# Modulation sums over 128 columns, and a new order of the first steps, in a decoder trunk

## Chip, cores and metric

One core of one Trainium2 chip. The metric is the device time of one execution in microseconds (us), as the median over runs.

## What is computed

One layer of a decoder trunk over 512 positions of 1024 channels: a modulated RMS norm, one input projection that feeds two attention branches, a gated merge, then a second modulated norm and a gated MLP. The change touches only the beginning, the modulated norm and the first 768 columns of the projection:

```python
cs = jax.nn.silu(c)
mod = cs @ w_ada[l] + b_ada[l]
shift1, scale1, gate1, shift2, scale2, gate2 = [m[:, None, :] for m in jnp.split(mod, 6, axis=-1)]
h = _rmsnorm(x, norm1_g[l]) * (1.0 + scale1) + shift1
proj = h @ w_in[l]
```

Here `x` is 512 x 1024, `c` is 1 x 1024, `w_ada` is 1024 x 6144 and `w_in` is 1024 x 4352, all float32. So each of the 1024 channels needs one scale and one shift before it can go into the projection, and each of these is a sum over 1024 products of `cs` with a column of `w_ada`.

## The kernel before

The 1024 channels are cut into eight blocks of 128, k = 0 to 7, and each block is one step. For a step the kernel needs `mod` (a scale and a shift for each of the 128 channels), the modulated tile `h` (128 channels x 512 positions), and the block's 128 x 768 weights. To keep float32 accuracy in a fast format, both operands are split into a high and a low part. `hTh` and `hTl` are the parts of `h`; `w0h` and `w0l` are those of the weights. A step multiplies high by high, low weight by high, and high by low `h`, for each of six output blocks (the six PSUM accumulators `acc6`).

*TensorE's order.* The instructions of TensorE, VectorE and ScalarE in this stage run in the order in which the program writes them (a manual schedule, L243). `mm_k(k, 0)` (L385) does the twelve products that need `hTh`; `mm_k(k, 2)` does the six that need `hTl`. Between them stands the work for the next step: reducing the modulation sums (`reduce_mod`, L314), transposing the next block of `x` (`h_turn`, L367), finishing `mod` (`finish_mod`, L325) and making the next `hTh` and its float32 copy `hf` (`h_tile`, L372). In step 1 the six products of `mm_k(1, 2)` are split in two halves of three, with the next step's work in between (L478).

*How a modulation sum is made.* `adaw[k]` holds the block of `w_ada` of step k: index j = 0 for the scale and j = 1 for the shift, and eight column blocks kk of 128 inputs. There are two ways. `direct` (L295) multiplies on TensorE: the 128 x 128 block of `adaw` is the weight, one column of `cs` is the moving operand, and the result is one column of PSUM. The other way runs on VectorE: `ac_first` (L272) and `ac_ops` (L281) multiply the blocks by their `cs` value and add them up, elementwise over 128 x 256, into two accumulators `ac` (even and odd kk), which are added at last. `reduce_mod` then sums `ac` over the partitions with a product by a column of ones.

Step 0 uses `direct` for all of the scale and for half of the shift; the other half of the shift, `a0`, is summed on VectorE (L434 to L438). Step 1 does kk = 6 and 7 directly (`early_mod`, L305) into columns 2 and 3 of a PSUM tile, VectorE adds these to the biases (`part`, L311), and the rest comes by `ac`. Steps 2 to 7 go all by `ac`. The `ac` of step k+1 is made while step k's products run.

*VectorE's list within a step* is: `ac_ops` for the next step with `h_low` (L382, which makes `hTl`) at some place in it, then `finish_mod`, then the two instructions of `split_lo` (L357, which make `w0l` of the next step). `ac_first` runs on ScalarE, apart from the odd one of step 2.

*Warmers.* `keep_warm(n)` (L254) multiplies the identity by ones into an accumulator that is overwritten later. It takes n x 128 columns, up to 512 in one product. Its only purpose is to keep TensorE busy.

*Loads.* SP's queue holds all loads of this stage in program order (L225): four tiles of `x` of 512 KB, then for each step the two 512 KB halves of `adaw` (in four pieces of 256 KB for steps 1 and 2) and 384 KB of `w_in`. Buffers of `adaw` are used again three or two steps later, so the issues of the last steps wait until VectorE has read the old contents. After this stage come further loads for the projections and for the rest of the modulation (`ra`, L834).

Of the kernel before, what the change touches and what calls it, by code (L numbers as in the profile page):

```python
# [39 lines left out]
DIFF_FILL = (3, 2, 4, 2)  # L40
WARM_EARLY = 5
WARM = 10
GROUPS = ((0,), (1,), (2,), (3,), (4,), (5,), (6,), (7,))
MOD_AT = 2

COL_KA = 512
COL_VA = 640
# [8 lines left out]
def kernel(  # L56
# [142 lines left out]
    p1 = ExitStack()  # L199
    pp = pool("p1", stack=p1)  # L200
    xn = pp.tile([P, NT, D], F32, name="xn")
    groups = GROUPS
    adaw, w0 = {}, {}

    def load_ada(g):
        k, m = g[0], len(g)
        if k % 3 == 2:
            aw = big.tile([P, 2, KT, m * P], F32, tag="out" + "hl"[k // 3], name=f"adaw{k}")
        else:
            aw = pp.tile([P, 2, KT, m * P], F32, tag="adaw", bufs=2, name=f"adaw{k}")  # L210
        cut = 4 if k in (1, 2) else KT
        for a in range(0, KT, cut):
            for j, base in ((0, D), (1, 0)):
                nc.sync.dma_start(
                    aw[:, j, a : a + cut],
                    wada[a * P : (a + cut) * P, base + k * P : base + (k + m) * P].rearrange("(a p) n -> p a n", p=P),
                )
        adaw[k] = aw

# [5 lines left out]
    with tc.manual_schedule(engines={nc.sync.engine}):  # L225
        for t in range(NT):
            nc.sync.dma_start(xn[:, t], xd[t * P : (t + 1) * P, :])
        load_ada(groups[0])
        load_w0(0)
        for k in range(1, KT):  # L230
            load_ada(groups[k])
# [38 lines left out]


    def ac_first(gi, b):  # L272
        a = pp.tile([P, 2, len(groups[gi]) * P], F32, tag=f"ac{b}", bufs=2, name=f"ac{gi}_{b}")
        aw = adaw[groups[gi][0]]
        if gi == 2 and b:
            nc.vector.tensor_scalar_mul(a, aw[:, :, b], cs[:, b : b + 1])
        else:
            nc.scalar.activation(a, aw[:, :, b], AF.Copy, scale=cs[:, b : b + 1])
        ac.setdefault(gi, {})[b] = a

    def ac_ops(gi, low):  # L281
        aw = adaw[groups[gi][0]]
        order = (3, 2, 5, 4) if gi == 1 else (3, 2, 5, 4, 7, 6)
        if gi == 2:
            ac_first(2, 1)
        for n, kk in enumerate(order):
            if n == (2, 4)[gi > 1] and gi < 3:
                low()
            a = ac[gi][kk % 2]
            nc.vector.scalar_tensor_tensor(a, aw[:, :, kk], cs[:, kk : kk + 1], a, ALU.mult, ALU.add)  # L290
        nc.vector.tensor_add(ac[gi][0], ac[gi][0], ac[gi][1])
        if gi > 2:
            low()

    def direct(pa, j, c, k, kks, stop=True):  # L295
        for kk in kks:
            nc.tensor.matmul(
                pa[:, c : c + 1],
                adaw[k][:, j, kk],
                cs[:, kk : kk + 1],  # L300
                start=kk == kks[0],
                stop=stop and kk == kks[-1],
            )

    def early_mod(gi):  # L305
        pa = tbank(f"pa{gi}", (P, 4))
        for c, j in ((2, 1), (3, 0)):
            direct(pa, j, c, gi, (6, 7))
        part = pp.tile([P, 2], F32, name="part")
        both = cols[:, 0:16].rearrange("p (a b) -> p b a", a=2)  # L310
        nc.vector.tensor_add(part, pa[:, 2:4], both[:, gi])  # L311
        return pa, part

    def reduce_mod(gi, early=None):  # L314
        pas = []
        for i, k in enumerate(groups[gi]):
            pa = early[0] if early else tbank(f"pa{k}", (P, 2))
            for j in range(2):
                nc.tensor.matmul(
                    pa[:, j : j + 1], ac[gi][0][:, j, i * P : (i + 1) * P], ones[:, 0:1], start=True, stop=True  # L320
                )
            pas.append(pa)
        return pas

    def finish_mod(gi, pas, early=None):  # L325
        for k, pa in zip(groups[gi], pas):
            m = pp.tile([P, 16], F32, tag="mod", bufs=3, name=f"mod{k}")
            sh, sc = (early[1][:, 0:1], early[1][:, 1:2]) if early else (bsh[:, k : k + 1], bsc1[:, k : k + 1])
            last = nc.vector.scalar_tensor_tensor(m[:, 0:1], pa[:, 0:1], sc, n1g[:, k : k + 1], ALU.add, ALU.mult)
            if gi:  # L330
                nc.scalar.activation(m[:, 1:2], pa[:, 1:2], AF.Identity, bias=sh)
            else:
                nc.vector.tensor_add(m[:, 1:2], pa[:, 1:2], sh)
            mods[k] = m
        return last

    def w0_views(k):
# [34 lines left out]
    def h_tile(k):  # L372
        hf = pp.tile([P, S], F32, tag="hf", bufs=2, name=f"hf{k}")
        for dst in (hTh[k], hf):
            nc.scalar.activation(dst, pts[k], AF.Identity, bias=mods[k][:, 1:2], scale=mods[k][:, 0:1])
            if dst is not hf and k < 2:
                if k == 0:
                    ac_first(1, 1)
                ac_first(k + 1, 0)
        hfs[k] = hf  # L380

    def h_low(k):  # L382
        nc.vector.tensor_sub(hTl[k], hfs[k], hTh[k].bitcast(F32))

    def mm_k(k, part, some=DONE):  # L385
        wh, wl = wts[k]
        last = k == KT - 1
        if part == (2 if last else 1):
            return
        for i in some:  # L390
            for p in (1, 2) if last and part else (0, 1) if part == 0 and not last else (part,):
                lhs, rhs = ((wh, hTh), (wl, hTh), (wh, hTl))[p]
                nc.tensor.matmul(  # L393
                    acc6[i], lhs[:, i * P : (i + 1) * P], rhs[k], start=k == 0 and p == 0, stop=last and p == 2
                )
# [25 lines left out]
    pa0 = tbank("pa0", (P, 2))  # L421
# [16 lines left out]
    nc.tensor.matmul(pa0[:, 1:2], a0, ones[:, 0:1], start=False, stop=True)  # L438
# [10 lines left out]
    for gi, g in enumerate(groups):  # L449
        nxt = groups[gi + 1] if gi + 1 < len(groups) else ()  # L450

        for k in nxt:
            split_hi(k)

        if nxt:
            ac_ops(gi + 1, lambda: h_low(g[0]))
        else:
            h_low(g[0])
        if not nxt:
# [12 lines left out]
        for k in g:  # L472
            if k == 0:
                h_turn(1)
            for part in range(3):
                part_2 = DONE
                if part == MOD_AT and k == g[-1] and nxt:
                    if gi == 1:  # L478
                        mm_k(k, part, DONE[:3])
                        part_2 = DONE[3:]  # L480
                    early = early_mod(1) if gi == 0 else None
                    pas = reduce_mod(gi + 1, early)
                    if gi and gi + 2 < len(groups):
                        ac_first(gi + 2, 1)
                        ac_first(gi + 2, 0)
                    if len(nxt) == 1 and gi:
                        h_turn(nxt[0])
                    last_mod = finish_mod(gi + 1, pas, early)
                    for n in nxt:
                        split_lo(n, 0)  # L490
                        split_lo(n, 1)
                    for n in nxt:
                        if len(nxt) > 1:
                            h_turn(n)
                        h_tile(n)
                mm_k(k, part, part_2)
            if k == g[0]:
                for n in g[1:]:
                    h_low(n)
    man.close()  # L500
    p1.close()

# [1410 lines left out]
```

## Time and profile before

| | us |
|---|---|
| runs shown | 696.82, 699.29, 698.24 |
| median of them | 698.24 |
| the profiled execution, whole | 697.19 |
| its span on the core | 695.1 |

The page of the profile gives a busy time for each engine (PE is TensorE, PEld its weight loads, DVE VectorE, ACT ScalarE, POOL GpSimd, SP the queue that issues loads). A row of a timeline begins with the start and the length in us, then comes the engine, the line of the kernel, the operation, the tile written and the tiles read, the shape, and the number of instructions merged into the row. In brackets stands how long the engine was idle before, and what ended that. A float32 product appears as two records, one of a float32r operand as one. The granted clock is the share of full speed that the chip gave TensorE.

### The profile page before, as it was taken

The page shows a single profiled execution, that of the slowest core. Times are in us where ns is not written, and L with a number is a line of the kernel's source. Part 1 is how long each engine was busy: PE and PEld are TensorE (multiplying, and loading weights), DVE is VectorE, ACT ScalarE, POOL GpSimd, SP SyncE. Part 2 cuts the span into 40 slices and gives each one's busy share as a digit, 9 for nine tenths or more (in the row PEclk, how much of TensorE's full clock was granted, in tenths as well). Part 3 has the DMA queues.
Part 4 walks back from the last instruction along what each step waited for, and adds up shares of the span by engine and source line. Part 5 has one row for each costly group of instructions (what it writes and reads, how often), then busy time and mean ns, then how long its engine had stood idle before and what let it go on. Part 6 is the DMA issues. An engine that isn't in the chain of part 4 may idle for free.

```text
span 695.1 us, 11259 instructions
## 1 busy us (share of the span) xinstructions
PE 683.7 (98%) x4203; PEld 593.3 (85%) x4203; DVE 567.6 (82%) x1073; ACT 382.7 (55%) x687; POOL 82.9 (12%) x100
## 2 busy tenths in 40 slices
PE   8999999999999999999999999999999999999995
PEld 4787877777788888888889999999999999888885
DVE  4799987887885557663789998888888999979997
ACT  6666675544552333332468756655555666655665
POOL 3000000000101000000030111111111102540300
PEclk9999999999999999999999999999999999999998
DMA  9984454454435676339817788787889648997903
GB/s 308 344 237 155 150 158 146 127 165 116 140 92 171 194 218 203 98 99 284 279 37 147 152 202 196 165 197 200 196 220 227 159 132 216 191 202 199 167 1 121
DMA packets 115926, 121.81 MB, mean 175 GB/s; under 512 B 4447, under 2 KB 93344, under 8 KB 115872
## 3 DMA queue, kind: packets, MB, share of 16 engines
q1 hardware_dynamic: 96958, 95.09, 43.6%
q0 software_dynamic: 18720, 25.73, 22.0%
q8 instruction: 33, 0.54, 0.3%
q10 hardware_dynamic: 194, 0.28, 0.1%
q14 instruction: 21, 0.17, 0.1%
HBM read 118.97 MB, written 2.11 MB: 174 GB/s over the span
## 4 chain that ended last, share of the span: by engine, by line
PE 91%; DVE 3%; DMA 3%; ACT 1%; issue 1%; SPq 0%; POOLq 0%; ACTq 0%; DVEq 0%
PE up L1242 32%; PE dc L1857 15%; PE a L393 4%; PE pgd L123 2%; PE oc L1298 2%; PE oc L1302 2%; PE pgd L125 2%; PE pgd L124 2%; PE oc L1299 2%; DMA ra<-in_w_ada_dram 2%; PE pga L123 2%; PE pga L125 2%; PE pga L124 2%; PE pw L123 1%; PE pk L123 1%; PE pk L125 1%
## 5 line engine op out<-in xcount | busy, mean ns | idle before, releaser
L1242 PE MATMUL up<-t,m_whi 128*128 128x256 f32 x512 | 93.1, 283 | 0.0
L1242 PEld LDWEIGHTS up<-t,m_whi 128*128 128x128 f32 x512 | 79.9, 192 | 0.0
L1242 PE MATMUL up<-t,m_wlo 128*128 128x256 f32 x256 | 72.4, 283 | 0.0
L1242 PE MATMUL up<-bh,p_whi 128*128 128x256 f32 x232 | 65.7, 283 | 0.0
L1242 PE MATMUL up<-bl,p_whi 128*128 128x256 f32 x232 | 65.7, 283 | 0.0
L1242 PE MATMUL up<-bh,p_wlo 128*128 128x256 f32 x232 | 65.7, 283 | 0.0
L858 DVE SCALAR_TENSOR_TENSOR arow<-ra,cs,arow 128x512 f32<-128x512 f32 x56 | 41.9, 749 | 21.6 <-DMA ra<-in_w_ada_dram 21.0
L1242 PEld LDWEIGHTS up<-t,m_wlo 128*128 128x128 f32 x256 | 49.2, 192 | 0.0
L1242 PEld LDWEIGHTS up<-bh,p_whi 128*128 128x128 f32 x232 | 44.5, 192 | 0.0
L1242 PEld LDWEIGHTS up<-bl,p_whi 128*128 128x128 f32 x232 | 44.5, 192 | 0.0
L1242 PEld LDWEIGHTS up<-bh,p_wlo 128*128 128x128 f32 x232 | 44.5, 192 | 0.0
L1151 POOL DMA_DIRECT2D s<-in_w_up_dram x21 | 27.0, 1361 | 139.6 <-DMA s<-in_w_up_dram 69.2
L1179 ACT CAST m_whi<-s 128x1024 fp32r<-128x1024 f32 x31 | 32.4, 1047 | 11.1 <-DVE s L1173 7.7
L1183 DVE TENSOR_TENSOR m_wlo<-s,m_whi 128x1024 fp32r<-128x1024 f32 x31 | 37.7, 1217 | 0.0
L1242 PE MATMUL up<-t,p_whi 128*128 128x256 f32 x176 | 32.2, 283 | 0.0
L877 POOL DMA_DIRECT2D mod_rows<-row x8 | 5.1, 643 | 197.0 <-ACT row L876 197.0
L177 POOL TENSOR_TENSOR r<-ms,mhalf 128x1 f32<-128x1 f32 (+1 forms) x16 | 13.1, 822 | 127.6 <-DVE ms L175 72.8
L772 ACT ACTIVATE sd<-sd,dmx 128x128 f32<-128x128 f32 (+3 forms) x32 | 17.7, 557 | 19.0 <-DVE dmx L764 18.9
L1242 PEld LDWEIGHTS up<-t,p_whi 128*128 128x128 f32 x176 | 27.5, 192 | 0.0
L1249 ACT ACTIVATE gT<-a,cv 128x512 f32<-128x512 f32 x22 | 17.7, 813 | 16.9 <-DVE a L1284 15.8
L1179 ACT CAST p_whi<-wa 128x1024 fp32r<-128x1024 f32 x18 | 18.7, 1041 | 12.6 <-PE up L1242 12.6
L1183 DVE TENSOR_TENSOR p_wlo<-wa,p_whi 128x1024 fp32r<-128x1024 f32 x18 | 22.0, 1220 | 3.8 <-ACT p_whi L1179 3.2
(491 smaller groups left out, 2077.9 us busy)
## 6 DMA issues: line engine op xcount, KB each, us to landing
ra<-in_w_ada_dram SPq DMA_DIRECT2D x32, 512.0 KB, 4.1
wa<-in_w_up_dram SPq DMA_DIRECT2D x22, 512.0 KB, 4.1
s<-in_w_up_dram SPq DMA_DIRECT2D x21, 512.0 KB, 4.6
s<-in_w_up_dram POOLq DMA_DIRECT2D x21, 512.0 KB, 6.7
adaw<-in_w_ada_dram SPq DMA_DIRECT2D x12, 512.0 KB, 6.5
w<-in_w_in_dram SPq DMA_DIRECT2D x12, 512.0 KB, 4.6
a<-in_w_up_dram SPq DMA_DIRECT2D x11, 512.0 KB, 4.5
b<-in_w_down_dram SPq DMA_DIRECT2D x10, 512.0 KB, 4.0
```

The lines of the kernel that those rows point to most:

```text
L123: nc.tensor.matmul(o, lh, rh, start=start, stop=False)
L124: nc.tensor.matmul(o, lh, rl, start=False, stop=False)
L125: nc.tensor.matmul(o, ll, rh, start=False, stop=stop)
L393: nc.tensor.matmul(acc6[i], lhs[:, i * P : (i + 1) * P], rhs[k], start=k == 0 and p == 0, stop=last and p == 2)
L772: exp = nc.scalar.activation(pm[m], pm[m], AF.Exp, bias=mx[:, m : m + 1], scale=slope, accum_out=lsum[:, m : m + 1])
L858: nc.vector.scalar_tensor_tensor(ac, r[:, a], cc, ac, ALU.mult, ALU.add)
L1151: nc.gpsimd.dma_start(dst, upblock(*blk), accum_op=ALU.add)
L1179: nc.scalar.copy(W[J, name][0], R[J, SRC[name]])
L1183: nc.vector.tensor_sub(lo, R[J, SRC[name]], hi.bitcast(F32))
L1242: nc.tensor.matmul(o[u], w[:, k, cu], b[:, k], start=name in ("p1", "m5", "p2") and k == 0 and x == 0, stop=k == 3 and x == 2, skip_group_ ...
L1249: nc.scalar.activation(grow(j), av[J][:, u], AF.Identity, bias=cv[:, 66 + j : 67 + j], scale=cv[:, 44 + j : 45 + j])
L1857: nc.tensor.matmul(bank2[u][:, sl], a[:, q, cu], b[:, q, sl], start=first_mm and x == 0, stop=last_mm and x == 2, skip_group_check=name no ...
```

## The change

Four things are done. First, `direct` uses its column of `cs` 128 times over (a broadcast, so the same column is read again), and the result is 128 equal columns of PSUM, of which the first is used; the same holds for `a0` and for step 1's reduction, which now multiply by all 128 columns of `ones`. Second, step 1's direct products and its reduction accumulate in the same PSUM columns, so `part` goes away. Third, step 0's direct products are laid out otherwise on TensorE: three of them ahead of the third transpose, five behind it and ahead of the fourth; and the warmer behind them has 256 columns instead of 512. Fourth, VectorE's list of the first steps: the odd `ac_first` of step 1 moves there from ScalarE; `w0l` of step 1 is made ahead of `finish_mod(1)`; in step 2's sums the order of kk is 3, 5, 2, 7, 4, 6, and `h_low(1)` comes behind them. With that, `mm_k(1, 2)` is no longer split in halves. The general case of steps with more than one block (`GROUPS`), which was not in use, is taken out.

```diff
     def ac_first(gi, b):
...
-        if gi == 2 and b:
+        if gi in (1, 2) and b:
             nc.vector.tensor_scalar_mul(a, aw[:, :, b], cs[:, b : b + 1])
...
     def ac_ops(gi, low):
-        aw = adaw[groups[gi][0]]
-        order = (3, 2, 5, 4) if gi == 1 else (3, 2, 5, 4, 7, 6)
-        if gi == 2:
-            ac_first(2, 1)
+        aw = adaw[gi]
+        if gi < 3:
+            ac_first(gi, 1)
+        order = {1: (3, 2, 5, 4), 2: (3, 5, 2, 7, 4, 6)}.get(gi, (3, 2, 5, 4, 7, 6))
         for n, kk in enumerate(order):
-            if n == (2, 4)[gi > 1] and gi < 3:
+            if gi == 1 and n == 2:
                 low()
...
-        if gi > 2:
+        if gi > 1:
             low()
...
-    def direct(pa, j, c, k, kks, stop=True):
+    def direct(pa, j, k, kks, start=True, stop=False):
         for kk in kks:
             nc.tensor.matmul(
-                pa[:, c : c + 1],
+                pa[:, j],
                 adaw[k][:, j, kk],
-                cs[:, kk : kk + 1],
-                start=kk == kks[0],
+                cs[:, kk : kk + 1].to_broadcast([P, P]),
+                start=start and kk == kks[0],
                 stop=stop and kk == kks[-1],
             )
...
     def early_mod(gi):
-        pa = tbank(f"pa{gi}", (P, 4))
-        for c, j in ((2, 1), (3, 0)):
-            direct(pa, j, c, gi, (6, 7))
-        part = pp.tile([P, 2], F32, name="part")
-        both = cols[:, 0:16].rearrange("p (a b) -> p b a", a=2)
-        nc.vector.tensor_add(part, pa[:, 2:4], both[:, gi])
-        return pa, part
+        pa = tbank(f"pa{gi}", (P, 2, P))
+        direct(pa, 0, gi, (6, 7))
+        return pa
...
     def reduce_mod(gi, early=None):
...
+        pa = early or tbank(f"pa{gi}", (P, 2, P))
+        for j in range(2):
+            if early:
+                if j:
+                    direct(pa, 1, gi, (6, 7))
+                nc.tensor.matmul(pa[:, j], ac[gi][0][:, j], ones, start=False, stop=True)
             else:
...
+                nc.tensor.matmul(pa[:, j, 0:1], ac[gi][0][:, j], ones[:, 0:1], start=True, stop=True)
+        return pa
...
         if t:
             normalise(t - 1)
+            if t == 3:
+                direct(pa0, 0, 0, range(3))
             turn(t - 1)
             if t < 3:
                 keep_warm(4)
     normalise(NT - 1)
-    direct(pa0, 0, 0, 0, range(7), False)
+    direct(pa0, 0, 0, range(3, 8), start=False, stop=True)
     turn(NT - 1)
-    nc.tensor.matmul(pa0[:, 0:1], adaw[0][:, 0, 7], cs[:, 7:8], start=False, stop=True)
...
-    direct(pa0, 1, 1, 0, range(4), False)
-    nc.tensor.matmul(pa0[:, 1:2], a0, ones[:, 0:1], start=False, stop=True)
-    finish_mod(0, [pa0])
+    direct(pa0, 1, 0, range(4))
+    nc.tensor.matmul(pa0[:, 1], a0, ones, start=False, stop=True)
+    finish_mod(0, pa0)
...
-    keep_warm(4)
+    keep_warm(2)
     h_tile(0)
...
         for dst in (hTh[k], hf):
             nc.scalar.activation(dst, pts[k], AF.Identity, bias=mods[k][:, 1:2], scale=mods[k][:, 0:1])
             if dst is not hf and k < 2:
-                if k == 0:
-                    ac_first(1, 1)
                 ac_first(k + 1, 0)
...
+        mm_k(gi, 0)
+        mm_k(gi, 1)
+        if more:
+            if gi == 0:
+                split_lo(1, 0)
+                split_lo(1, 1)
+            pa = reduce_mod(gi + 1, early_mod(1) if gi == 0 else None)
+            if gi and gi + 2 < KT:
+                ac_first(gi + 2, 1)
+                ac_first(gi + 2, 0)
+            if gi:
+                h_turn(gi + 1)
+            last_mod = finish_mod(gi + 1, pa)
+            if gi:
+                split_lo(gi + 1, 0)
+                split_lo(gi + 1, 1)
+            h_tile(gi + 1)
+        mm_k(gi, 2)
```

More of the change, by code (lines that the diff above doesn't have):

```diff
@@ L201, with load_ada @@
     xn = pp.tile([P, NT, D], F32, name="xn")
-    groups = GROUPS
     adaw, w0 = {}, {}
-    def load_ada(g):
-        k, m = g[0], len(g)
+    def load_ada(k):
         if k % 3 == 2:
-            aw = big.tile([P, 2, KT, m * P], F32, tag="out" + "hl"[k // 3], name=f"adaw{k}")
+            aw = big.tile([P, 2, KT, P], F32, tag="out" + "hl"[k // 3], name=f"adaw{k}")
         else:
-            aw = pp.tile([P, 2, KT, m * P], F32, tag="adaw", bufs=2, name=f"adaw{k}")
+            aw = pp.tile([P, 2, KT, P], F32, tag="adaw", bufs=2, name=f"adaw{k}")
         cut = 4 if k in (1, 2) else KT
@@ L215, in load_ada @@
                     aw[:, j, a : a + cut],
-                    wada[a * P : (a + cut) * P, base + k * P : base + (k + m) * P].rearrange("(a p) n -> p a n", p=P),
+                    wada[a * P : (a + cut) * P, base + k * P : base + (k + 1) * P].rearrange("(a p) n -> p a n", p=P),
                 )
@@ L227 @@
             nc.sync.dma_start(xn[:, t], xd[t * P : (t + 1) * P, :])
-        load_ada(groups[0])
+        load_ada(0)
         load_w0(0)
         for k in range(1, KT):
-            load_ada(groups[k])
+            load_ada(k)
             load_w0(k)
@@ L272, in ac_first @@
     def ac_first(gi, b):
-        a = pp.tile([P, 2, len(groups[gi]) * P], F32, tag=f"ac{b}", bufs=2, name=f"ac{gi}_{b}")
-        aw = adaw[groups[gi][0]]
-        if gi == 2 and b:
+        a = pp.tile([P, 2, P], F32, tag=f"ac{b}", bufs=2, name=f"ac{gi}_{b}")
+        aw = adaw[gi]
+        if gi in (1, 2) and b:
             nc.vector.tensor_scalar_mul(a, aw[:, :, b], cs[:, b : b + 1])
@@ L281, in ac_ops @@
     def ac_ops(gi, low):
-        aw = adaw[groups[gi][0]]
-        order = (3, 2, 5, 4) if gi == 1 else (3, 2, 5, 4, 7, 6)
-        if gi == 2:
-            ac_first(2, 1)
+        aw = adaw[gi]
+        if gi < 3:
+            ac_first(gi, 1)
+        order = {1: (3, 2, 5, 4), 2: (3, 5, 2, 7, 4, 6)}.get(gi, (3, 2, 5, 4, 7, 6))
         for n, kk in enumerate(order):
-            if n == (2, 4)[gi > 1] and gi < 3:
+            if gi == 1 and n == 2:
                 low()
@@ L305, in early_mod, with finish_mod @@
     def early_mod(gi):
-        pa = tbank(f"pa{gi}", (P, 4))
-        for c, j in ((2, 1), (3, 0)):
-            direct(pa, j, c, gi, (6, 7))
-        part = pp.tile([P, 2], F32, name="part")
-        both = cols[:, 0:16].rearrange("p (a b) -> p b a", a=2)
-        nc.vector.tensor_add(part, pa[:, 2:4], both[:, gi])
-        return pa, part
-    def reduce_mod(gi, early=None):
[L315 to L331, printed above, removed]
-            else:
-                nc.vector.tensor_add(m[:, 1:2], pa[:, 1:2], sh)
-            mods[k] = m
+        pa = tbank(f"pa{gi}", (P, 2, P))
+        direct(pa, 0, gi, (6, 7))
+        return pa
+    def reduce_mod(gi, early=None):
+        pa = early or tbank(f"pa{gi}", (P, 2, P))
[4 more added lines that the diff above has]
+                nc.tensor.matmul(pa[:, j], ac[gi][0][:, j], ones, start=False, stop=True)
+            else:
+                nc.tensor.matmul(pa[:, j, 0:1], ac[gi][0][:, j], ones[:, 0:1], start=True, stop=True)
+        return pa
+    def finish_mod(k, pa):
+        m = pp.tile([P, 16], F32, tag="mod", bufs=3, name=f"mod{k}")
+        last = nc.vector.scalar_tensor_tensor(
+            m[:, 0:1], pa[:, 0, 0:1], bsc1[:, k : k + 1], n1g[:, k : k + 1], ALU.add, ALU.mult
+        )
+        if k:
+            nc.scalar.activation(m[:, 1:2], pa[:, 1, 0:1], AF.Identity, bias=bsh[:, k : k + 1])
+        else:
+            nc.vector.tensor_add(m[:, 1:2], pa[:, 1, 0:1], bsh[:, k : k + 1])
+        mods[k] = m
         return last
@@ L383, in h_low, with mm_k @@
         nc.vector.tensor_sub(hTl[k], hfs[k], hTh[k].bitcast(F32))
-    def mm_k(k, part, some=DONE):
+    def mm_k(k, part):
         wh, wl = wts[k]
@@ L389, in mm_k @@
             return
-        for i in some:
+        for i in DONE:
             for p in (1, 2) if last and part else (0, 1) if part == 0 and not last else (part,):
@@ L419, in scale_x @@
         nc.scalar.activation(xn[:, t, HEAD:], xn[:, t, HEAD:], AF.Copy, scale=rst[:, t : t + 1])
-    pa0 = tbank("pa0", (P, 2))
+    pa0 = tbank("pa0", (P, 2, P))
     for t in range(NT):
@@ L447 @@
     split_lo(0, 1)
[L449 to L456, printed above, removed]
-        else:
-            h_low(g[0])
-        if not nxt:
+    for gi in range(KT):
+        more = gi + 1 < KT
+        if more:
+            split_hi(gi + 1)
+            ac_ops(gi + 1, lambda: h_low(gi))
+        else:
+            h_low(gi)
             lp = cpool.tile([P, 2, 64], F32, name="lp")
@@ L470 @@
             nc.vector.tensor_scalar_add(nlam, nlam, -LAM_INIT)
[L472 to L499, printed above, removed]
+        if gi == 0:
+            h_turn(1)
+        mm_k(gi, 0)
+        mm_k(gi, 1)
+        if more:
+            if gi == 0:
+                split_lo(1, 0)
[12 more added lines that the diff above has]
+        mm_k(gi, 2)
     man.close()
```

2 lines of the change are left out of this document (removed).

## The prediction

> **What bounds the kernel now.** I read the page first, then the busy times in stretches, then TensorE's timeline of the first 40 us, then VectorE's and ScalarE's.
>
> ```profile
> span 695.1 us, 11259 instructions
> PE 683.7 (98%) x4203; PEld 593.3 (85%) x4203; DVE 567.6 (82%) x1073; ACT 382.7 (55%) x687; POOL 82.9 (12%) x100
> ```
>
> TensorE is busy for 98% of the span. The question is where it is idle, or busy at less than full speed. The stretches (columns: stretch, its length, then busy us of PE, PEld, DVE, ACT and POOL, granted clock, DMA share, GB/s):
>
> ```profile
> 10.76:14.17 3.41, 3.34 (x28) 2.77 (x26) 2.61 (x9) 3.07 (x5) 0.62 (x1) 1.00 1.12 363
> 14.17:17.58 3.41, 3.41 (x11) 2.27 (x11) 2.14 (x7) 2.31 (x5) 0.00 (x0) 0.50 1.12 365
> 60.00:690.00 630.00, 626.95 (x3941) 550.31 (x3940) 521.47 (x950) 340.41 (x610) 76.47 (x75) 1.00 0.64 165
> ```
> ```profile
> 687.47 0.28 PE L1857 MATMUL dc<-p4wh,p4a 128*128 128x256 f32 x1
> ```
>
> From 60 to 690 us TensorE misses 3 us of 630, and 2.25 of them lie behind its last product (687.47 + 0.28). So what comes earlier into that stretch comes out earlier by as much. The second row is the loss: for 3.41 us the clock is at half. The stretch just before it looks 98% busy, but what fills it are products of one column:
>
> ```profile
> 10.31 1.02 PE L258 MATMUL a<-ones,ident 128*128 128x512 f32 x2
> 11.57 1.62 PE L297 MATMUL pa<-cs,adaw 128*128 128x1 f32 x14
> 13.34 1.09 PE L297 MATMUL pa<-cs,adaw 128*128 128x1 f32 x8
> 14.29 0.57 PE L438 MATMUL pa<-ones,a 128*128 128x1 f32 x2
> 14.72 2.05 PE L258 MATMUL a<-ones,ident 128*128 128x512 f32 x2
> 16.57 1.06 PE L370 MATMUL xt<-ident,xn 128*128 128x128 f32 x4
> 17.28 0.61 PE L393 MATMUL a<-hThA,w0h 128*128 128x512 f32 x1
> 17.73 0.39 PE L393 MATMUL a<-hThA,w0l 128*128 128x512 f32 x1
> 17.96 0.39 PE L393 MATMUL a<-hThA,w0h 128*128 128x512 f32 x1
> 20.25 0.95 PE L297 MATMUL pa<-cs,adaw 128*128 128x1 f32 x8
> 21.45 0.61 PE L319 MATMUL pa<-ones,ac 128*128 128x1 f32 x4 [0.25 <-DVE part L311]
> 21.91 1.64 PE L393 MATMUL a<-hTlA,w0h 128*128 128x512 f32 x6
> 23.47 0.50 PE L393 MATMUL a<-hThA,w0h 128*128 128x512 f32 x1
> 27.21 0.58 PE L319 MATMUL pa<-ones,ac 128*128 128x1 f32 x4
> 29.22 0.51 PE L393 MATMUL a<-hThA,w0h 128*128 128x512 f32 x1 [0.23 <-ACT hThA L375]
> 34.31 0.39 PE L393 MATMUL a<-hThA,w0h 128*128 128x512 f32 x1
> 39.34 0.50 PE L393 MATMUL a<-hThA,w0h 128*128 128x512 f32 x1
> ```
>
> The two 512-column warmers take 1.02 us at 10.31 and 2.05 us at 14.72: the same instructions at half the clock. The modulated tile that the first real product needs was there before TensorE was free:
>
> ```profile
> 15.28 0.78 ACT L375 ACTIVATE hThA<-xt,mod 128x512 fp32r<-128x512 f32 x1 [1.16 <-DVE mod L333]
> ```
>
> It is ready at 15.28 + 0.78 = 16.06, and TensorE starts on it at 17.28: late by 1.2 us, behind warmers and transposes at half clock.
>
> [...]
>
> **The change part by part.** A float32 product leaves two records. The direct sums get 128 columns instead of one: 26 records for step 0 (24 of adaw, 2 of a0), 8 direct and 4 reducing for step 1, 38 in all. One-column records now follow each other at about (1.09 - 0.31) / 7 = 0.11 us, the time of their weight loads. No row shows a float32 product with a repeated column as moving operand. Bounds from the nearest rows:
>
> ```profile
> 32.45 0.63 PE L370 MATMUL xt<-ident,xn 128*128 128x128 f32 x4
> 32.84 1.63 PE L393 MATMUL a<-hTlA,w0h 128*128 128x512 f32 x6
> L297 PEld LDWEIGHTS pa<-cs,adaw 128*128 128x128 f32 x30 | 3.8, 196 | 0.1
> ```
>
> From below, four 128-column transposes with four different weights take 32.84 - 32.45 = 0.39, 0.10 each. From above, a weight load of 0.196 that hides behind nothing comes on top of the 0.11. The two 512-column records above follow each other by about 0.43 at full clock, so 128 columns stream in 0.107, which fits inside the load. I take 0.11, that is no cost, and keep +0.196 for the range.
>
> [...]
>
> *Step 0.* Three of the direct products go ahead of the third transpose, so TensorE starts them at about 11.2, when the warmers have streamed (the trace names no wait on their weights' load at 11.57; were they that late, the step would lose at most 0.35). 26 records at 0.11 and two transposes at 0.15 put the last start at 14.25 and its end at 14.5, against 14.29 + 0.57 = 14.86. From there to the tile the rows give 16.06 - 14.86 = 1.20, so hTh of step 0 is ready at 15.7. TensorE meanwhile has one warmer of 256 columns (2 x 0.21) and four transposes (0.4, after the mod at about 14.9): done by 15.3, it waits. If the clock holds, the twelve products start at 15.75 and take 12 x 0.23 = 2.77: they end at 18.5 instead of 20.25. That is 1.75, and nearly all of it is the clock.
>
> *Step 1.* From 20.25 to 21.91 TensorE does 8 direct records, waits for VectorE's `part` and reduces: 1.66 us.
>
> ```profile
> 19.06 0.42 DVE L291 TENSOR_TENSOR ac<-ac,ac 128x256 f32<-128x256 f32 x1
> 21.23 0.16 DVE L311 TENSOR_TENSOR part<-pa,cols 128x2 f32<-128x2 f32 x1 [1.74 <-PE pa L297]
> 22.23 0.68 DVE L361 TENSOR_TENSOR w0l<-w,w0h 128x512 fp32r<-128x512 f32 x1
> 22.82 0.42 DVE L363 TENSOR_TENSOR w0l<-w,w0h 128x256 fp32r<-128x256 f32 x1
> 23.16 0.35 DVE L276 TENSOR_SCALAR ac<-adaw,cs 128x256 f32<-128x256 f32 x1
> 22.64 0.78 ACT L375 ACTIVATE hThA<-xt,mod 128x512 fp32r<-128x512 f32 x1
> ```
>
> Now the sums stay in PSUM, `part` and its wait go, and 12 records take 1.33. What VectorE's sums take:
>
> ```profile
> 16.48 0.88 DVE L290 SCALAR_TENSOR_TENSOR ac<-adaw,cs,ac 128x256 f32<-128x256 f32 x2 [0.37 <-ACT ac L278]
> 17.55 0.69 DVE L383 TENSOR_TENSOR hTlA<-hf,hThA 128x512 fp32r<-128x512 f32 x1 [0.18 <-ACT hf L375]
> ```
>
> VectorE's list of step 1 gains one multiplication by a scalar (0.35, taken off ScalarE) and is ready with `ac` at about 18.85: it starts 15.8 after w0l of step 0, then 0.35, two sums 0.83, hTl 0.61, two sums 0.83 and the add 0.4. TensorE asks at 18.5 + 0.45 = 18.95, so this is hidden by 0.1 us; every further 0.1 would show. The two w0l of step 1 (1.01 us) go into the 1.74 us in which VectorE now waits, and cost nothing there. The reduction's end to the next tile is the old chain, 23.47 - (21.45 + 0.61) = 1.41. It ends at 20.05, so step 1's products start at 21.45 against 23.47: 2.0 gained by then, 0.25 more than after step 0.
>
> *Step 2.* From 23.47 to 29.22 step 1 takes 5.75; a later step takes 39.34 - 34.31 = 5.03. The excess of 0.72 is the reduction at 27.21, which waited for `ac`, and the wait for hThA at 29.22. VectorE is now free 0.9 earlier in this step (no w0l), so its 8 operations end 3.5 after mod, at 23.8, and hTl at 24.45. TensorE asks for `ac` at 24.2 and for hTl at 25.0. So hTl may stand last on VectorE's list and the products need not be split in two. I take the whole 0.72. Sum: 1.75 + 0.25 + 0.72 = 2.7 us.
>
> *What is late next.* The loads do not come earlier: the DMA share is 1.12 in both stretches above. Step 3's and step 2's weights are the tightest:
>
> ```profile
> 13.23 2.53 SPq L214 DMA_DIRECT2D adaw<-in_w_ada_dram  x4
> 17.36 1.54 SPq L214 DMA_DIRECT2D adaw<-in_w_ada_dram  x2
> 25.20 0.91 ACT L278 ACTIVATE ac<-adaw,cs 128x256 f32<-128x256 f32 x2
> ```
> ```profile
> DMA to landing us min/median/max: 4.7/5.3/7.8
> ```
>
> ScalarE used them at 25.20 without a wait. Now it reaches them at about 23.4, ahead of mod and hTh of step 2, which queue behind them on ScalarE. The second of their two loads is issued at about 18.1; by the median it lands at 23.4, at the latest at 25.2, where it was used. TensorE needs hTh at 26.4 (21.45 + 5.0); mod 0.3 and hTh 0.8 behind 0.9 of `ac` allow a landing up to 24.4. At the latest, 25.2, TensorE loses 0.8. I take 0. Step 2's last quarter, issued at about 15.0, lands at 20.3 by the median; the new order asks for it (column block 5, now ahead of 2, which needs a product of ScalarE's) at 20.9, with 0.4 in hand at `ac`. SP issues step 6's and 7's weights when VectorE has released step 3's and 4's, so those move with VectorE.
>
> The span should fall from 695.1 to 692.4. The profiled execution took 697.19, so 694.5 by its own time; the median of the runs shown, 698.24, is 1.05 higher and becomes 695.5. That is the forecast.
>
> **The rivals.** (a) *The clock was whole in most timed executions of before.* One profile shows one fall. With the clock whole, the old order would have hTh at about 15.8, and step 0 gains nothing; 0.25 + 0.72 remain: 697.3. [...]
>
> (b) *The clock falls all the same*: a repeated column counts like one. Then one warmer (0.85) and the transposes (0.85) at half clock end at 16.3, and products run at half rate to 17.58, which loses 0.64 more: 1.2 of the 2.7 is lost, 697.0. Against it: the stretch at half clock holds warmers and 128-column transposes, and the clock returned after it.
>
> (c) *Step 3's weights land last* and take 0.8: 696.3.
>
> (d) *Slower: weight loads and wide products do not overlap.* All 38 records lie on the path, each dearer by up to 0.196: +7.4 - 2.7 = +4.7, 702.9. It decides from 2.7 / 38 = 0.07 us a record. The rows of line 393 speak against it; for it, that float32 loads of distinct weights beside equally long streams stand nowhere in the trace at full clock except as transposes.
>
> **How the numbers follow.** Forecast 0.55, (a) 0.18, (b) 0.10, (c) 0.10, (d) 0.07. The range 693.9 to 697.6 runs from the forecast less the spread of the runs (1.4 below the median, taken whole with some more) to just over (a), and leaves out (d) and the far ends. About 0.3%, 2.1 us here, is what a measurement can tell from no change; the forecast of 2.7 is close above it. Faster: nearly all of the forecast and a part of (c) and (b), 0.60. Same: (a), most of (b) and (c), and the milder half of (d), 0.34. Slower 0.06.
>
> **What would show it.** Right: granted clock 1.00 from 10 to 20 us; the records of the 128-column sums 0.11 apart; the first product of line 393's group near 15.75, step 1's near 21.4, step 2's near 26.4; no wait for `part` and none for hThA before step 2; from 60 us on the same order 2.7 us earlier. Wrong: a stretch at half clock still in the first 20 us, records 0.2 apart or more, a wait of ScalarE for adaw that reaches hThA, or a shift at 30 us that is gone at 100.

## The result, and the profile after

| | before | after |
|---|---|---|
| median, runs side by side | 697.35 (696.59 to 699.29, 6 runs) | 693.98 (693.65 to 694.66, 6 runs) |
| profiled execution, whole | 697.19 | 694.24 |
| its span | 695.1 | 692.1 |

The ratio is 0.9949, with an interval of 0.9934 to 0.9963: 3.4 us faster, where 2.7 were forecast (695.5 was forecast for the median). The page of the changed kernel, and its stretches (columns as before):

```profile
span 692.1 us, 11257 instructions
PE 681.9 (99%) x4203; PEld 593.0 (86%) x4203; DVE 568.2 (82%) x1073; ACT 382.5 (55%) x686; POOL 82.9 (12%) x100
```
```profile
10.76:14.17 3.41, 3.41 (x27) 2.93 (x26) 2.74 (x11) 3.11 (x5) 0.62 (x1) 1.00 1.11 356
14.17:17.58 3.41, 3.22 (x19) 2.35 (x18) 2.72 (x8) 2.49 (x5) 0.00 (x0) 1.00 1.11 364
57.00:687.00 630.00, 627.61 (x3943) 550.55 (x3941) 522.08 (x950) 340.64 (x610) 76.44 (x75) 1.00 0.64 165
```

In the stretch from 14.17 to 17.58 the granted clock is now 1.00, where it was 0.50. TensorE's timeline of the first steps:

```profile
10.64 1.02 PE L254 MATMUL a<-ones,ident 128*128 128x512 f32 x2
11.50 0.83 PE L293 MATMUL pa<-cs,adaw 128*128 128x128 f32 x6
...
12.28 1.28 PE L293 MATMUL pa<-cs,adaw 128*128 128x128 f32 x10
...
13.51 1.06 PE L293 MATMUL pa<-cs,adaw 128*128 128x128 f32 x8
14.40 0.39 PE L429 MATMUL pa<-ones,a 128*128 128x128 f32 x2
14.62 0.60 PE L254 MATMUL a<-ones,ident 128*128 128x256 f32 x2
15.25 0.63 PE L362 MATMUL xt<-ident,xn 128*128 128x128 f32 x4
16.03 0.50 PE L383 MATMUL a<-hThA,w0h 128*128 128x512 f32 x1 [0.15 <-ACT hThA L367]
...
18.89 0.60 PE L293 MATMUL pa<-cs,adaw 128*128 128x128 f32 x4
19.34 0.39 PE L312 MATMUL pa<-ones,ac 128*128 128x128 f32 x2
19.56 0.61 PE L293 MATMUL pa<-cs,adaw 128*128 128x128 f32 x4
20.00 0.39 PE L312 MATMUL pa<-ones,ac 128*128 128x128 f32 x2
20.15 1.62 PE L383 MATMUL a<-hTlA,w0h 128*128 128x512 f32 x6
21.81 0.50 PE L383 MATMUL a<-hThA,w0h 128*128 128x512 f32 x1
...
24.70 0.50 PE L314 MATMUL pa<-ones,ac 128*128 128x1 f32 x4
...
26.92 0.39 PE L383 MATMUL a<-hThA,w0h 128*128 128x512 f32 x1
...
31.86 0.40 PE L383 MATMUL a<-hThA,w0h 128*128 128x512 f32 x1
```

Eight records from 13.51 to 14.40 are 0.111 apart. The products of the first three steps begin at 16.03, 21.81 and 26.92 instead of 17.28, 23.47 and 29.22. The only wait named is 0.15 for the first modulated tile; those for `part` and for step 2's tile are gone. On the other two engines, in step 2, the rows on which its timing hung:

```profile
24.02 0.42 DVE L287 TENSOR_TENSOR ac<-ac,ac 128x256 f32<-128x256 f32 x1
24.36 0.68 DVE L373 TENSOR_TENSOR hTlA<-hf,hThA 128x512 fp32r<-128x512 f32 x1
```
```profile
24.40 0.91 ACT L274 ACTIVATE ac<-adaw,cs 128x256 f32<-128x256 f32 x2 [0.76 <-DMA adaw<-in_w_ada_dram]
25.50 0.26 ACT L323 ACTIVATE mod<-pa,cols 128x1 f32<-128x1 f32 x1 [0.19 <-DVE mod L319]
25.80 0.78 ACT L367 ACTIVATE hThA<-xt,mod 128x512 fp32r<-128x512 f32 x1
```

The low part of `h` ends at 25.04, ahead of TensorE's use of it behind the transposes. ScalarE does wait for step 3's weights, 0.76 us, but then waits again for `mod` and has the tile at 26.58, before 26.92. Further on, rows of TensorE's timeline, first before, then after:

```profile
58.58 0.48 PE L123 MATMUL pq<-hThA,w_h 128*128 128x512 f32 x1
...
63.41 0.96 PE L130 MATMUL sw<-ka,qa 64*128 64x256 f32 x11 [0.40 <-DVE mx L633]
...
141.83 0.30 PE L790 MATMUL td<-ident,sd 128*128 128x128 f32 x1 [0.31 <-DVE dls L775]
```
```profile
55.98 0.48 PE L121 MATMUL pq<-hThA,w_h 128*128 128x512 f32 x1
...
684.48 0.28 PE L1834 MATMUL dc<-p4wh,p4a 128*128 128x256 f32 x1
```

The first product behind the stage is 2.60 us earlier (58.58 to 55.98), the last of all 2.99 (687.47 to 684.48). Between them lie two waits of before, 0.40 at 63 us and 0.31 at 142 us, that the rows of after at these places do not name; they are more than the 0.4. So one execution against the other gives 3.0, and the medians 3.4. The missing 0.4 must lie in the other runs; those of before differ more than those of after, and experiment 1 asks why.

### The profile page after: what moved, and what is told of

The parts are those of the page before. It is cut to its first block, busy times and chain, and to the rows that moved or that the text cites. A ratio compares the mean times of both kernels' runs of the same rounds, so it can differ in the third digit from the quotient of the medians.

```text
span 692.1 us, 11257 instructions
## 1 busy us (share of the span) xinstructions
PE 681.9 (99%) x4203; PEld 593.0 (86%) x4203; DVE 568.2 (82%) x1073; ACT 382.5 (55%) x686; POOL 82.9 (12%) x100
## 4 chain that ended last, share of the span: by engine, by line
PE 97%; DMA 1%; DVE 0%; ACT 0%; issue 0%; POOLq 0%; ACTq 0%; DVEq 0%
PE up L1219 32%; PE dc L1834 15%; PE a L383 5%; PE pga L121 2%; PE pgd L121 2%; PE oc L1275 2%; PE pga L123 2%; PE pga L122 2%; PE oc L1279 2%; PE pgd L123 2%; PE oc L1276 2%; PE pgd L122 2%; PE sd L128 1%; PE pw L121 1%; PE pA L121 1%; PE pk L121 1%
```

## The experiments

Every ratio is against the kernel before, run on the same chip.

**1. The kernel before, once more** (no edit), to see what its executions do.

> The kernel before, once more. Theory 1 (one-column sums lose the clock): again a stretch at half clock of about 3.4 us somewhere between 12 and 19 us, mean granted clock of its runs near 0.994 like the first profile; and TensorE idle about 0.4 us near 63 us only if the load of ra lands late again. Rival (a) (the clock is whole in most executions): no such stretch, mean clock 0.997, the first product of step 0 near 15.8. Time against before: none, within 0.15%.

It measured 0.9991 (0.9974 to 1.0009), and its runs scatter from 695.15 to 698.73. The profile took 698.44, and these are its stretches and TensorE's timeline:

```profile
10.15:13.56 3.41, 3.05 (x21) 2.23 (x21) 2.74 (x11) 3.06 (x6) 0.89 (x2) 1.00 1.08 351
13.56:16.97 3.41, 3.41 (x15) 2.89 (x15) 1.34 (x6) 1.48 (x3) 0.00 (x0) 0.50 1.12 364
16.97:20.39 3.42, 3.42 (x11) 2.41 (x10) 2.84 (x7) 3.30 (x7) 0.00 (x0) 0.50 1.13 363
```
```profile
10.60 1.02 PE L258 MATMUL a<-ones,ident 128*128 128x512 f32 x2
...
11.86 1.62 PE L297 MATMUL pa<-cs,adaw 128*128 128x1 f32 x14
...
15.84 2.06 PE L258 MATMUL a<-ones,ident 128*128 128x512 f32 x2
17.68 1.06 PE L370 MATMUL xt<-ident,xn 128*128 128x128 f32 x4
18.39 0.78 PE L393 MATMUL a<-hThA,w0h 128*128 128x512 f32 x1
```

Here the clock is at half for two such stretches, 6.83 us, and the first product starts at 18.39, 1.11 later than in the profile of before. The warmers at the start of the rows stand 0.29 later than there (10.60 against 10.31), the fall 0.61 earlier (13.56 against 14.17): the place of the fall in the work differs between these two executions of one kernel. In the first stretch at half clock, one-column products fill the first two thirds (13.56 to 15.84), and the clock did not return after it, though TensorE was busy for all of it (3.41 of 3.41).

Each run shows its mean granted clock, in which one stretch of 3.41 us at half clock weighs 0.5 x 3.41 / 695 = 0.0025; the profile of before with its one stretch has 0.994, this one 0.992. Runs without a fall show 0.996 to 0.998, not 1, as the end of an execution, behind the last products, is at half clock too (0.50 from 690 to 692 us in the profile of after). So the runs can be sorted. All runs of the kernel before whose clock is on record (this one's ten, and those beside the experiments, on three chips), and three other kernels:

| kernel | runs with two stretches at half: median | with one | with none |
|---|---|---|---|
| before, 94 runs | 32: 698.39 (697.90 to 699.06) | 48: 696.70 (696.13 to 697.97) | 14: 695.18 (694.90 to 695.40) |
| after, 1 column (3.) | 7: 696.51 (695.53 to 696.76) | 2: 695.00, 695.19 | 1: 693.87 |
| after, 8 columns in step 0 (11.) | 2: 697.16, 697.63 | 5: 696.03 (695.46 to 696.82) | 3: 693.96 to 694.83 |
| after, 6 runs | none | none | 6: 693.98 (693.65 to 694.66) |

A stretch at half costs the kernel before about 1.6 us, and 80 of 94 runs had at least one; on the three chips 7 of 41, 4 of 24 and 3 of 29 runs kept the clock. (0.992 and 0.993 are taken as two, 0.994 and 0.995 as one, 0.997 and more as none. The value 0.996 does not tell by itself: the only run of before that has it, 696.97, is taken as one by its time; the runs with it of after and of experiments 2, 5 and 7 are as short as the others of their kernel, and count as none. In experiments 6 and 10 the longest run has it, 696.04 and 696.72, which stays undecided.)

**2. Before, with 128 columns in step 0's sums alone.** `wide(j, kks)` is `direct` with `cs[:, kk : kk + 1].to_broadcast([P, P])` into `pa0[:, j]`, in before's order.

```diff
-    direct(pa0, 0, 0, 0, range(7), False)
+    wide(0, range(7))
...
-    nc.tensor.matmul(pa0[:, 0:1], adaw[0][:, 0, 7], cs[:, 7:8], start=False, stop=True)
+    wide(0, (7,), True)
...
-    direct(pa0, 1, 1, 0, range(4), False)
-    nc.tensor.matmul(pa0[:, 1:2], a0, ones[:, 0:1], start=False, stop=True)
+    wide(1, range(4))
+    nc.tensor.matmul(pa0[:, 1], a0, ones, start=False, stop=True)
```

> The kernel before, with only step 0's direct sums and a0 over 128 columns; order, warmers and steps 1 and 2 as before. Theory 1: no half clock before 600 us, records 0.11 apart, first product of step 0 near 16.0 instead of 17.3 (the 512-column warmer and the transposes end at about 15.9), 1.4 to 1.7 us faster (ratio 0.9976 to 0.998). Rival (b) (a repeated column counts like one): half clock stays, time within 0.3 us of before.

It measured 695.27, ratio 0.997 (0.9959 to 0.9981), with a mean clock of 0.996 to 0.998 in all ten runs. TensorE's timeline:

```profile
13.52 1.28 PE L425 MATMUL pa<-cs,adaw 128*128 128x128 f32 x10
14.64 0.39 PE L445 MATMUL pa<-ones,a 128*128 128x128 f32 x2
14.86 1.02 PE L258 MATMUL a<-ones,ident 128*128 128x512 f32 x2
...
16.27 0.50 PE L393 MATMUL a<-hThA,w0h 128*128 128x512 f32 x1
```

The warmer takes 1.02 again, where it took 2.05 in the profile of before, and the ten records are 0.112 apart. The median is that of before's runs without a fall (695.27 and 695.18): the wide sums give the clock and nothing else, and any cost of theirs is too small for the medians to show. With this, rivals (b) and (d) are out.

**3. After, with one column everywhere.**

```diff
-                pa[:, j],
+                pa[:, j, 0:1],
                 adaw[k][:, j, kk],
-                cs[:, kk : kk + 1].to_broadcast([P, P]),
+                cs[:, kk : kk + 1],
...
-                nc.tensor.matmul(pa[:, j], ac[gi][0][:, j], ones, start=False, stop=True)
+                nc.tensor.matmul(pa[:, j, 0:1], ac[gi][0][:, j], ones[:, 0:1], start=False, stop=True)
```

> The changed kernel with its direct sums, a0 and step 1's reduction over one column, everything else of the change kept. Theory 1: the half clock comes back, mean clock 0.994, the first product starts between 16.0 and 16.5 and runs at half rate until the stretch ends, 1.2 to 1.8 us slower than the changed kernel (ratio to before 0.9965 to 0.998). Rival (order and shorter lists do it all): same time as the changed kernel, 0.995.

It measured 696.17, ratio 0.9978 (0.9961 to 0.9996). Nine of ten runs had stretches at half clock (table), seven of them two, as its profile had:

```profile
13.74:17.15 3.41, 3.41 (x15) 3.12 (x15) 2.17 (x7) 2.23 (x5) 0.00 (x0) 0.50 1.12 361
17.15:20.57 3.42, 3.42 (x9) 2.65 (x9) 3.26 (x8) 1.96 (x4) 0.00 (x0) 0.50 1.12 363
```

The one run that kept the clock took 693.87, the time of after. By this one run, and by experiment 2, all that 128 columns bring is the clock, and the new order is worth the rest.

**4. After, with step 0 as before** (old order, long warmer, and `narrow`, which is `direct` with one column).

```diff
-            if t == 3:
-                direct(pa0, 0, 0, range(3))
...
-    direct(pa0, 0, 0, range(3, 8), start=False, stop=True)
+    narrow(0, range(7))
     turn(NT - 1)
+    narrow(0, (7,), True)
...
-    keep_warm(2)
+    keep_warm(4)
```

> The changed kernel with step 0 as before (one column, old order, 512-column warmer); steps 1 and 2 as changed. Theory: half clock as before, first product of step 0 near 17.3; from there 0.25 us gained up to step 1's products and 0.7 up to step 2's, so 1.0 us faster (ratio 0.9986), up to 1.5 if the stall near 63 us goes with it. Rival (only the clock counts): within 0.3 us of before.

It measured 696.54, ratio 0.9997 (0.9983 to 1.0011), and is no clean answer. The fourth step begins at 33.57, 0.74 before that of before (34.31), but the end of the stage loses it again: the first product behind it starts at 58.70, against 58.58 in before. What lies outside the hand-written lists was ordered otherwise there:

```profile
53.47 0.24 PE L517 MATMUL pcv<-ident,crow 88*128 88x88 f32 x1
53.98 1.66 PE L383 MATMUL a<-hThB,w0h 128*128 128x512 f32 x6 [0.28 <-ACT hThB L367]
```

In after the `pcv` transpose stands behind the last step (at 55.96) and that wait does not exist. The next run puts the same question without this difference.

**5. After, with step 0's old order and warmer, but 128 columns.** The edit is that of 4 with `direct` in place of `narrow`.

> The changed kernel with step 0's old order and 512-column warmer, sums over 128 columns everywhere: the kernel of the run with wide sums alone, plus the changed steps 1 and 2. Its clock should be whole in every run, so the two compare closely. Theory: steps 1 and 2 are worth 0.25 + 0.72 by the profile, up to 1.0 us: 694.2 against 695.25; step 2's products start near 27.1 instead of 28.15. Rival (all of the gain is the clock): 695.25, step 2's start near 28.

It measured 694.53, ratio 0.9972 (0.9962 to 0.9982), clock 0.996 to 0.998 in all runs. Against 2 it differs in steps 1 and 2 alone: 0.74 by the medians. By TensorE's timeline:

```profile
22.08 0.50 PE L383 MATMUL a<-hThA,w0h 128*128 128x512 f32 x1
...
27.20 0.40 PE L383 MATMUL a<-hThA,w0h 128*128 128x512 f32 x1
```

In 2 these starts are 22.39 and 28.15, with the same step 0: 0.31 by step 1, 0.95 by step 2, and 1.24 at the first product behind the stage (56.30 against 57.54). The two medians come from two chips; the runs of before without a fall have medians of 695.15 and 695.30 there, so that the chips differ by little.

**6. Before, with all of step 0 changed**: 2, and the three products ahead of the third transpose, five behind it, and the warmer of 256 columns.

```diff
+            if t == 3:
+                wide(0, range(3))
             turn(t - 1)
...
-    wide(0, range(7))
+    wide(0, range(3, 8), True)
     turn(NT - 1)
-    wide(0, (7,), True)
...
-    keep_warm(4)
+    keep_warm(2)
```

> The kernel before with all of step 0 as changed (128 columns, three products ahead of the third transpose, 256-column warmer), steps 1 and 2 as before. Theory: 0.2 us better than the wide sums alone (first product near 16.03 instead of 16.27), so 695.0, mean clock 0.997 in every run. Rival (the new order of step 0 is worth the 0.35 that was forecast for it): 694.9 and a start at 15.9. Rival (steps 1 and 2 do nothing): time of the changed kernel, 694.0.

It measured 695.05, ratio 0.9979 (0.9968 to 0.9989). Its first product starts at 15.91 against 16.27 in 2: the order of step 0 is worth 0.36 in the profile and 0.22 by the medians, the latter within what the runs scatter.

**7, 8 and 11. After, with 32, 64 or 8 columns in step 0's sums.**

```diff
+        n = P if k else 32
         for kk in kks:
             nc.tensor.matmul(
-                pa[:, j],
+                pa[:, j, 0:n],
                 adaw[k][:, j, kk],
-                cs[:, kk : kk + 1].to_broadcast([P, P]),
+                cs[:, kk : kk + 1].to_broadcast([P, n]),
```

> The changed kernel with step 0's direct sums and a0 over 32 columns. [...] Rival (any width above one counts as busy): clock whole, 0.997 in all runs, 694.0.

> [...]

> The changed kernel with step 0's direct sums and a0 over 8 columns. 32 columns kept the clock in all ten runs, one column lost it in nine of ten. [...] If lost, mean clock 0.992 to 0.995 in most runs and 695 to 697; if kept, 0.996 to 0.998 in all and 694.5.

64 columns measured 693.8, ratio 0.9957, clock 0.997 to 0.998. 32 columns measured 694.5, ratio 0.9961, and kept the clock too, 0.996 to 0.998 in all ten runs: I had expected them to lose it, and that was wrong. (In its profile the end of the stage comes 0.89 later than in after, 56.87, with a wait of 0.66 for a tile of the last step, as 8 columns also have it; but the last product is only 0.10 later, at 684.58. So the half microsecond that its median lies over that of after is not explained.) 8 columns measured 695.93, ratio 0.9977 (0.9963 to 0.9991), and seven of ten runs had one or two stretches at half clock (table). TensorE's timeline with 32 columns:

```profile
12.19 1.20 PE L294 MATMUL pa<-cs,adaw 128*128 128x32 f32 x10
...
13.37 0.98 PE L294 MATMUL pa<-cs,adaw 128*128 128x32 f32 x8
```

Eight records from 13.37 to 14.19 are 0.10 apart there (128 columns: 0.111); with 8 columns, eight from 13.60 to 14.41 are 0.10 apart too, and in both profiles TensorE's timeline names no idle time in these rows. So what keeps the clock here lies between 8 columns, with three runs of ten, and 32, with ten of ten. What it is about the wider products that keeps it is not shown, and no limit beyond these rows follows.

**9. After, with w0l of step 1 behind its mod, as before.**

```diff
-            if gi == 0:
-                split_lo(1, 0)
-                split_lo(1, 1)
             pa = reduce_mod(gi + 1, early_mod(1) if gi == 0 else None)
...
-            if gi:
-                split_lo(gi + 1, 0)
-                split_lo(gi + 1, 1)
+            split_lo(gi + 1, 0)
+            split_lo(gi + 1, 1)
```

> The changed kernel with step 1's w0l behind its mod again, as before. Theory: VectorE's 1.01 us then stand between mod and step 2's sums, which end at 25.4 instead of 24.4; TensorE asks for them at 24.7 and waits 0.7: step 2's products start near 27.6 instead of 26.9, 694.7. Rival (VectorE has that much in hand): start at 26.9, 694.0.

TensorE's timeline:

```profile
25.18 0.58 PE L314 MATMUL pa<-ones,ac 128*128 128x1 f32 x4 [0.34 <-DVE ac L287]
...
27.48 0.39 PE L383 MATMUL a<-hThA,w0h 128*128 128x512 f32 x1
```

With w0l behind mod, VectorE ends `ac` late, TensorE waits 0.34 for it, and step 2's products start at 27.48 instead of 26.92. The profiled execution is 0.41 longer than that of after (694.65 and 694.24). The median is not settled by that: it is 695.91, ratio 0.9985 (0.9968 to 1.0003), since five runs lie at 694.65 to 695.36 and five at 696.47 to 699.33, and the clock explains at most two of these (698.55 with 0.994 and 699.33 with 0.995, a clock like that of a run with a stretch at half, in spite of 128 columns; the others have 0.996 and 0.997). No profile shows such a run, and what lengthens them stays open.

**10. After, with the old order of step 2's sums, `h_low(1)` among them again, and the six products of step 1 in two halves.**

```diff
-        order = {1: (3, 2, 5, 4), 2: (3, 5, 2, 7, 4, 6)}.get(gi, (3, 2, 5, 4, 7, 6))
+        order = (3, 2, 5, 4) if gi == 1 else (3, 2, 5, 4, 7, 6)
...
+            if gi == 1:
+                mm_k(gi, 2, DONE[:3])
             pa = reduce_mod(gi + 1, early_mod(1) if gi == 0 else None)
...
-        mm_k(gi, 2)
+        mm_k(gi, 2, DONE[3:] if gi == 1 else DONE)
```

> The changed kernel with step 2's old order of sums, hTl of step 1 within them and its products in two halves of three. Theory: ac is ready at about 24.9, the reduction stands behind three products at 25.4, and hTh of step 2 comes at 27.4 for a TensorE that is done at 26.9: 0.45 us later, 694.4. Rival (w0l ahead of mod was all): start at 26.9, 694.0.

```profile
26.43 0.94 PE L383 MATMUL a<-hTlA,w0h 128*128 128x512 f32 x3
27.61 0.51 PE L383 MATMUL a<-hThA,w0h 128*128 128x512 f32 x1 [0.23 <-ACT hThA L367]
```

On TensorE's timeline the wait of 0.23 for step 2's tile is back, as in before, and the step starts at 27.61, 0.69 later than after; its step 1 started 0.14 later, so the order is worth 0.55. The median, 695.54, ratio 0.9974 (0.996 to 0.9988), is 1.6 above that of after. In the profile the fourth step is 0.85 later than in after (32.71 against 31.86), a wait of 0.33 for a tile at 48 us adds to it, and the first product behind the stage is 1.58 later (57.56 against 55.98).

**12. After, without the warmer behind the second transpose**, as a version that might beat both: step 0's direct sums would start earlier.

```diff
-            if t < 3:
+            if t == 1:
                 keep_warm(4)
```

> The changed kernel without the warmer behind the second transpose, so that the direct products start when their weights have landed (10.8) instead of at 11.5. Theory: step 0's sums are one unbroken row on TensorE, so its products start 0.5 to 0.65 earlier (15.4), unless step 3's weights, which land at 24.3, now hold hTh of step 2: then 0.3 of it is kept, 693.4 to 693.7 in the end, clock whole. Rival (the warmer is needed for the clock): mean clock 0.995 or less in some runs. Rival (landing of x or VectorE bounds step 0): no gain.

```profile
10.32 0.93 PE L293 MATMUL pa<-cs,adaw 128*128 128x128 f32 x6 [0.28 <-DMA adaw<-in_w_ada_dram]
...
15.05 0.50 PE L383 MATMUL a<-hThA,w0h 128*128 128x512 f32 x1
```

On TensorE's timeline the first product starts at 15.05, 0.98 before that of after, and the direct sums now wait for their weights' load. The span is 691.2, 0.9 shorter. But the median is 694.19 (693.11 to 695.71), ratio 0.9952 (0.9935 to 0.9969) beside 0.9949: no gain is shown. All its runs kept the clock (0.996 to 0.998), so something else makes them scatter, and that stays open.

## Why the prediction was right in kind and short in size

*Step 0.* "If the clock holds" was an assumption, as no row of before has a repeated column, and it was right: in every run of after, and, as far as the mean clock tells, in every run with 32 columns or more but the two of experiment 9. The records are 0.11 apart as taken, so no product is dearer, and a weight load (0.196, the mean of the 30 in before) did not come on top of each: 0.111 is little more than the 0.107 put for 128 columns (an estimate, a quarter of the 0.43 between the 512-column records). The first product came at 16.03, not 15.75: the direct products began at 11.50, not "about 11.2", since the warmers ahead of them stood at 10.64 instead of 10.31. That is not the change: in the second profile of the old kernel they stand at 10.60. Counted as the prediction counts, at the end of the twelve products, step 0 gave 20.25 - 18.89 = 1.36 in this profile, not 1.75. The 0.23 taken for each of the twelve is what the rows of line 393 show (17.73 to 17.96); after's twelve took 18.89 - 16.03 = 2.86, 0.24 each.

*Step 1* was put at 0.25; it gave 23.47 - 21.81 = 1.66, less 1.36, that is 0.30, and 0.31 in experiment 5. *Step 2* was put at 0.72; it gave 29.22 - 26.92 = 2.30, less 1.66, that is 0.64, and the same in 5. Experiments 9 and 10 show that both edits are needed for it: without the one the wait for `ac` comes back, without the other that for the tile, and step 2 begins 0.56 or 0.55 later. "I take 0" for step 3's weights held: rival (c)'s wait is there, 0.76, but it ends before TensorE's need.

*The sum* of the stage was 2.7, and 2.60 was measured on the profiles. The three terms make 2.30 of it; 0.15 more came by the fourth step's start (34.31 - 31.86 = 2.45), mostly because the third step's first product no longer follows on a wait, and the rest further on. "What comes earlier into that stretch comes out earlier by as much" held between these two profiles but for 0.4, and two waits that differ between executions of the same kernel are enough for that: experiment 1 has no wait at 63 us and no named one at 143. It does not hold as a rule: 32 columns leave the stage 0.89 later than after and end 0.10 later.

*The step that failed* is the last of the sum: "The profiled execution took 697.19, so 694.5 by its own time; the median of the runs shown, 698.24, is 1.05 higher and becomes 695.5." That carries the offset of before's runs over to after as if it were scatter that both have. It was lost clock, as the table has it: a run near 698.2 is one with two stretches at half clock, which the change takes away whole. (The clocks of the six runs of before beside after are not on record; this is read from their times.) After's median is 0.26 below its profiled time, not 1.05 above it, and 1.05 + 0.26 = 1.31 is most of the 1.5 between 695.5 and 693.98. The term mis-sized is step 0's gain, "That is 1.75, and nearly all of it is the clock", read from one execution with one stretch at half clock. Over the 94 runs of before, one stretch costs 696.70 - 695.18 = 1.52 and two cost 698.39 - 695.18 = 3.21, so the mean is (48 x 1.52 + 32 x 3.21) / 94 = 1.87, and the six runs beside after had 697.35 - 695.18 = 2.17. The rest is the order: 695.18 - 693.98 = 1.20, where steps 1 and 2 were put at 0.97. The two make up the measured 3.37 by construction. What speaks for the split are experiment 2, where the clock alone brought the time to 695.27, and experiments 5 and 6, where the order on top of it gave 0.74 by steps 1 and 2 and 0.22 by step 0; the 0.24 left of the 1.20 is in neither.

*Rival (a)* had its mechanism right and its share wrong: "the clock was whole in most timed executions of before" is so in 14 of 94. In those the gain is 1.20, near its 0.97, which put step 0's order at nothing (0.36 in the profile of experiment 6). Where the clock falls differs between the two profiled executions of before, 14.17 and 13.56, and the one with a second stretch at half took 698.44 - 697.19 = 1.25 us longer. Why few runs escape, and why some have two stretches, no run shows. *Rival (b)* is priced at 697.0, but 695.5 + 1.2 is 696.7; it is out all the same.

## What to carry to other kernels

Where the clock falls in the middle of a kernel, look at the mean granted clock of every run, not only at the profile: when times lie in groups, here about 1.6 us apart, the profiled execution is a draw from several, and an edit that holds the clock is worth the mean over them. The rows of one-column products looked 98% busy here and still lost the clock; widening them with a repeated column, to 128 columns with the records still 0.111 apart, held it at no cost that a median shows. Judge an order by the starts of the steps in the trace, and keep in mind that a small edit can also change the order of work outside the hand-written lists.

## What the runs showed of the hardware

The clock can stay at half for a second stretch although TensorE was busy in all of the first: 13.56 to 16.97 of experiment 1, 3.41 of 3.41 us busy, 15 records, and 0.50 again up to 20.39. The profile of experiment 3 has the same, 13.74 to 17.15, 3.41 of 3.41 us busy, 15 records, and 0.50 again up to 20.57. One-column products filled two thirds of the first stretch in experiment 1; that they kept the clock down there is not shown apart.

Products narrower than 128 columns were enough: 32 columns, in records 0.10 apart, kept the clock in ten runs of ten; 8 columns, in records as far apart, kept it in only three of ten, and one column in one of ten (experiments 7, 11 and 3). A moving operand that is one column read 128 times kept it too, in every run of experiment 2 (ten, 0.996 to 0.998) and of after (six, 0.996 and 0.997).
